# A one-token difference of attention values by way of DRAM, with regrouped stores of a triangular inverse

## The chip, the cores and the metric

The kernel runs on one NeuronCore of one Trainium2 chip. Its engines each work through a queue of their own in order: PE (TensorE, matmul), DVE (VectorE), ACT (ScalarE), POOL (GpSimd) and SP (SyncE). DMAs are issued from the queues of SP, ACT and POOL. The metric is the device time of one launch in microseconds, as the median of several runs. A profile is one execution of its own, taken by the hardware profiler.

## The reference

One layer of a decoder trunk on a sequence of 1024 tokens, width 1024, all in float32. One projection of the normalised input feeds three branches, whose gated sum goes through an output projection and then a feed-forward block with a short causal convolution:

```python
h = rms_norm(x, norm1_g)
p_rwkv, p_sb, q_mem, gate_logits = split(h @ w_in)
y_a = rwkv7_branch(p_rwkv, ...)            # delta-rule recurrence, 8 heads of 64
y_b = stick_breaking_branch(p_sb, ...)     # causal attention, 8 heads of 64
y_m = memory_branch(q_mem, mem, ...)       # attention into 256 memory tokens
x = x + (sum over branches of sigmoid(gate) * (y @ w_branch)) @ w_out
x = x + conv_ffn(x)
```

In the second branch the weight of an earlier token is a product over the tokens between; with `z = q k / 8` the reference computes

```python
attn = where(mask, exp(log_sigmoid(z) + log_between), 0)
out  = attn @ v
```

The weights of one query sum to one less a running product of `sigmoid(-z)`. So the kernel doesn't form the weights but the running product itself, and multiplies it with the differences of neighbouring values, `v[t-1] - v[t]`; the value of the last token of each block of 128 is added at the end as a bias. These differences, and these last values, are what the change is about.

## The kernel before

**Matmul in three products.** Each operand that must be exact is split into a rounded part and a rest (`split_w`, `split_raw`): ACT writes the rounded part (L80), POOL the rest (L81), and PE runs three products (`mm3`, all recorded at L112, the line of the helper `mmul`; transposes are at L105). Weights come in tiles of 128x1024 (`wr`, L76, two buffers, from SP's queue), with two buffers each for the parts `wh` and `wl`.

**The order of the work.** `run` weaves a main stage with a stream of filler items. `items` is a list of generators; `stream` starts each one (its weight load and split) one item ahead and then steps through it. `weave` steps the main stage and draws fillers at a ratio. PE's instructions stay in the order in which they are written (`pinned`); the other engines' orders are set by a scheduler under priorities. The main stages are: `rwkv_prep(p)` for the four head pairs p, `sb_attn`, `mem_attn`, `stage2` (the recurrence), `group_norm`. After them come the output projection, the up phase and the down phase, whose products fill PE.

**Around the values.** While `rwkv_prep(3)` runs, the fillers are the eight items of `sb_v`: for two halves `jg` of the sequence and four weight tiles `kt`, 24 products each. After `kt == 3` ACT writes four blocks of 128 tokens x 512 columns to two tiles `raw` (tag `w4`, three buffers; L655), two token blocks e = 0, 1 to a tile. `differ(i, raw)` then makes the difference tile `v[i]` (tag `A`, four buffers): L622 copies rows 0 to 126 of `raw` to rows 1 to 127 of `v`, from SBUF to SBUF; L623 and L625 copy the single row 127 to row 0 of the next block; L626 stores row 127 to the DRAM tensor `vld`; and on DVE L627 subtracts `raw`. `load_vlast` (L668) brings the last values back as eight DMAs of single numbers, one for each half of the partitions and tile (`jk`), so that ACT can take them as a bias (L868).

In the same stretch `rwkv_prep(3)` needs DVE for its elementwise chains (L384 to L387), for the masked copies of Gram products out of PSUM (`gram`, L401) and for the first steps of the inverse, and PE for the Gram products and for transposes (`turned`, L423). PSUM tiles of tag `g` have four buffers. SP also carries the stores `scr` (L285, L405), `mad` (L409) and `ggd` (L436). POOL brings `mad` back as `inst` (L457).

**The inverse.** `inverse` solves 128 unit triangular systems of 64x64 in place, one to a partition of `X = inst`, in 124 DVE steps (L467, L469) that the fillers draw (`pace`). At the end one DMA from POOL's queue (L472) stores all of `inst` to the DRAM tensor `td`, 16 KB from each partition. The buffer of `inst` is used again for `yhi` (L1091) once that store has read it.

**The recurrence.** `stage2` goes through 16 chunks of 64 tokens, two to a group g. For each group SP loads, for each head pair, a tile of stored operands (`at<-scr`, L490), and for each two pairs a tile `V2` from `vd` (two DMAs, L494) and from `td` (four DMAs, L497, each 64 partitions x 2 x 64 numbers). The fillers there are the gate and branch projections, whose loads (`w<-yd` L1105, `w<-gsd` L1119, `w<-mrd` L1122, `wr`) stand in the same queue of SP.

Of the kernel before, what the change touches and what calls it, by code (L numbers as in the profile page):

```python
# [11 lines left out]
F32 = mybir.dt.float32  # L12
# [3 lines left out]
ALU = mybir.AluOpType  # L16
AX = mybir.AxisListType

T = 1024
# [3 lines left out]
NG = NC // 2  # L23
# [26 lines left out]
class Trunk:  # L50
# [67 lines left out]
    def setup(self):  # L118
        nc, tc = self.nc, self.tc
        E = self.ctx.enter_context  # L120
        self.pool_c = E(tc.tile_pool(name="const", bufs=1))
        self.bufs_p = {"mm": 4, "g": 4}
        self.pool_ps = E(tc.tile_pool(name="psum", bufs=4, space=bass.MemoryType.PSUM))
        self.pool_d = E(tc.tile_pool(name="dram", bufs=1, space=bass.MemoryType.DRAM))
        self.pool_wt = E(tc.tile_pool(name="weights", bufs=2))
        self.pool_s = E(tc.tile_pool(name="small", bufs=2))
        self.kon = self.pool_c.tile([128, NKON], F32, name="kon")
        self.params = self.pool_c.tile([128, NPAR], F32, name="params")
        nc.sync.dma_start(self.params, self.I["params"])

        def kon(n):
            o, w = KON[n]
            return self.kon[:, o : o + w]

        self.ident, self.blk, self.ones = kon("ident"), kon("blk"), kon("ones")
        self.mm_mask, self.ind = kon("mm"), kon("ind")
        self.scr = self.pool_d.tile([4, NG, 128, 1024], F32, name="scr")
        self.mad = self.pool_d.tile([128, 64, 64], F32, name="mad")
        self.vd = self.pool_d.tile([2, 2, NG, 64, 4, 64], F32, name="vd")
        self.td = self.pool_d.tile([128, 64, 64], F32, name="td")  # L140
        self.yd = self.pool_d.tile([3, 4, 128, 1024], F32, name="yd")
        self.mrd = self.pool_d.tile([8, 128, 1024], F32, name="mrd")
        self.gsd = self.pool_d.tile([3, 8, 128, 1024], F32, name="gsd")
        self.x2d = self.pool_d.tile([8, 128, 1024], F32, name="x2d")
        self.vmd = self.pool_d.tile([128, 1024], F32, name="vmd")
        self.vld = self.pool_d.tile([4, 1024], F32, name="vld")
        self.actd = self.pool_d.tile([NF // 2, 7, 128, 512], F32, name="actd")
        self.ggd = self.pool_d.tile([4, 2, 128, 1024], F32, name="ggd")

# [310 lines left out]
    def inverse(self):  # L460
        nc = self.nc
        X = self.inst
        for s in range(1, 63):
            n = 63 - s
            tmp = self.t4("it")
            tv = tmp[:, : s * n].rearrange("p (j t) -> p j t", j=s)
            self.pinned(nc.vector.tensor_tensor(tv, X[:, 0:s, s : s + 1].to_broadcast([128, s, n]), X[:, s : s + 1, s + 1 : 64].to_broadcast([128, s, n]), ALU.mult))  # L467
            yield
            self.pinned(nc.vector.tensor_tensor(X[:, 0:s, s + 1 : 64], X[:, 0:s, s + 1 : 64], tv, ALU.add))  # L469
            yield  # L470
        nc.vector.memset(X.rearrange("p s t -> p (s t)")[:, 0 : 64 * 64 : 65], 1.0)
        nc.gpsimd.dma_start(self.td, X)  # L472

    def stage2(self):
        nc = self.nc
# [5 lines left out]
        hq = [slice(0, 64), slice(64, 128)]  # L481
        heads = [(p, h2) for p in range(4) for h2 in range(2)]
# [4 lines left out]
        def load(g, p, what="LV"):  # L487
            if "L" in what:
                Ls[g, p] = self.t4("at")
                nc.sync.dma_start(Ls[g, p], self.scr[p, g])  # L490
            if "V" in what and p % 2 == 0:
                V2 = self.t4("qk")
                for h2 in range(2):
                    nc.sync.dma_start(V2[hq[h2], h2 * 256 : h2 * 256 + 256], self.vd[p // 2, h2, g].rearrange("s c i -> s (c i)"))  # L494
                td = self.td.rearrange("(p h g c) s i -> p h g s c i", p=4, h=2, g=NG)
                for i, h2 in heads[0:4]:
                    nc.sync.dma_start(V2[hq[h2], 512 + i * 128 : 640 + i * 128].rearrange("s (c i) -> s c i", c=2), td[p + i, h2, g])  # L497
                for i in range(2):
                    VTs[g, p + i] = [V2[:, h2 * 256 + i * 128 : h2 * 256 + i * 128 + 128] for h2 in range(2)], V2[:, 512 + i * 128 : 640 + i * 128]

# [7 lines left out]
        for c in range(NC):  # L508
            g, cc = c // 2, c % 2
# [104 lines left out]
    def sb_v(self):  # L614
        nc = self.nc
        out = {}
        self.v = []
        halves = [slice(0, 512), slice(512, 1024)]

        def differ(i, raw):  # L620
            v = self.v[i]
            nc.sync.dma_start(v[1:128], raw[0:127])  # L622
            nc.sync.dma_start(v[0:1, halves[1]], raw[127:128, halves[0]])  # L623
            if i < 3:
                nc.sync.dma_start(self.v[i + 1][0:1, halves[0]], raw[127:128, halves[1]])  # L625
            nc.sync.dma_start(self.vld[i : i + 1], raw[127:128])  # L626
            nc.vector.tensor_tensor(v, v, raw, ALU.subtract)  # L627

        def item(jg, kt):
            hi, lo = self.split_w(self.I["w_v"][kt])  # L630
            yield
            if kt == 0:
                out[jg] = [self.ps("mm") for _ in range(4)]
            if (jg, kt) == (0, 3):
                self.v += [self.t4("A", n=1024) for _ in range(4)]
                nc.vector.memset(self.v[0][0:1, halves[0]], 0.0)

            def mm(kk, j):
                k = kt * 2 + kk
                w = slice(kk * 512, (kk + 1) * 512)  # L640
                js = slice((jg * 4 + j) * 128, (jg * 4 + j + 1) * 128)
                for pi, (a, b) in enumerate(((self.xhi, hi), (self.xlo, hi), (self.xhi, lo))):
                    self.mmul(out[jg][j], a[k][:, js], b[:, w], start=(k == 0 and pi == 0), stop=(k == 7 and pi == 2))

            for i in range(4):
                for e in range(2):
                    if kt == 3:
                        mm(e, i)
                    else:
                        mm(i // 2, i % 2 * 2 + e)  # L650
                if kt == 3:
                    jj = jg * 4 + i
                    if i % 2 == 0:
                        raw = self.t4()
                    nc.scalar.activation(raw[:, (jj % 2) * 512 : (jj % 2 + 1) * 512], out[jg][i], AF.Copy, scale=self.rsc[:, jj : jj + 1])  # L655
                    if i % 2:
                        differ(jj // 2, raw)
                if i == 1:
                    self.settle()
                yield  # L660

        return [item(jg, kt) for jg in range(2) for kt in range(4)]

    def load_vlast(self):
        self.vlast = self.small("jk", [128, 64], bufs=1)[:, :32].rearrange("c (i u) -> c i u", i=4)
        for i in range(4):
            for e in range(2):
                self.nc.sync.dma_start(  # L668
                    self.vlast[e * 64 : e * 64 + 64, i], self.vld[i, e * 512 : e * 512 + 512].rearrange("(u c) -> c u", c=64))

    def head_norm(self, pst, nh, width, fold, neg=None):
        nc = self.nc
# [133 lines left out]
    def sb_attn(self, qk, need):  # L806
# [40 lines left out]
        def back(u):  # L847
# [13 lines left out]
            if b % 4 == 2:  # L861
                q = slice(h2 * 64, h2 * 64 + 64)
                y = self.t4("ys", n=512)
                for i in range(2):
                    rows = slice(i * 64, i * 64 + 64)
                    for bb in range(2):
                        o = (2 * bb + i) * 128
                        nc.scalar.activation(  # L868
                            y[q, o : o + 128], py[rows, bb * 128 : bb * 128 + 128], AF.Identity,
                            bias=self.vlast[rows, half * 2 + bb, 2 * p + h2 : 2 * p + h2 + 1])  # L870
                nc.scalar.dma_start(self.yd[1, p, q, half * 512 : (half + 1) * 512], y[q])

        for u in range(len(units) + 4):
# [817 lines left out]
    def run(self):  # L1691
# [16 lines left out]
        self.marks = marks  # L1708
        items = [self.shift_item(i + p, krv[p], f"{n}{p}") for p in range(4) for n, i in (("k", 4), ("r", 0), ("v", 8)) if (p, n) != (0, "k")]
        items += self.sb_v()  # L1710
        inv = self.inverse()
        gq = [(b, d) for b in (1, 0) for d in range(8)]
        gq[14:14] = [(2, 0), (2, 1)]
# [2 lines left out]
        mark = lambda name: lambda: marks.add(name)  # L1716
        for p in range(4):
            kp, kss, qp, hooks = self.sb_qk(p, qk[p])
            items += [kp, gate(), kss, qp, gate(hooks), mark(f"sb{p}")]
            if p == 0:  # L1720
                items.append(self.load_vlast)
        prep, mss, mv, mk = self.mem_kv()
        mqi = [None] * 4
        for h in range(4):
# [119 lines left out]
```

## Time and profile before

| | |
|---|---|
| median of 3 runs | 1969.23 us (1967.92 to 1970.93) |
| the profiled execution's own time | 1968.17 us |
| its span in the profile | 1966.4 us |
| mean granted TensorE clock | 0.972 of full speed |
| PE busy | 1836.3 us (93%) |
| PE weight loads busy | 1458.2 us (74%) |
| DVE / ACT / POOL busy | 1167.1 / 886.9 / 775.3 us |
| DMA | 259.19 MB, mean 132 GB/s |

The span is what the profile covers; the time of the execution is 1.77 us longer. PE is busy nearly throughout, so what matters are the stretches where it is not: idle time of an engine that PE doesn't wait for costs nothing. In the rows of a timeline, what stands in square brackets is the idle time of that engine just before the row and what ended it. In the rows of windows each engine has its busy time in the window and the number of its instructions; then come the granted clock, the busy share of the 16 DMA engines and their rate.

### The profile page before, as it was taken

The numbers are of one execution on the slowest core, as the hardware profiler recorded it, in microseconds if no ns is written. First come the engines' busy times: TensorE is split into PE (matmuls) and PEld (weight loads), VectorE is DVE, ScalarE is ACT, GpSimd is POOL, SyncE is SP. The second block draws the span as 40 slices with busy tenths as digits, with TensorE's granted clock in tenths as the row PEclk, the third lists the DMA queues.
The fourth block names the chain that finished last, engine by engine and source line by source line (L and its number), as shares of the span: only waits on it lengthen the run. The fifth ranks groups of instructions, "written<-read, shape, count | busy, mean of one in ns | idle before, by whom it ended". The sixth has DMA issues, their size and how long they took to land. (4 is left out here: it accounts for less than half of the span.)

```text
span 1966.4 us, 27535 instructions
## 1 busy us (share of the span) xinstructions
PE 1836.3 (93%) x10500; PEld 1458.2 (74%) x10500; DVE 1167.1 (59%) x1643; ACT 886.9 (45%) x1665; POOL 775.3 (39%) x432
## 2 busy tenths in 40 slices
PE   8999966499999999999899989989999999999999
PEld 6777755377878788777677768767888888878877
DVE  5756641388888632433423376266767777786496
ACT  5444411246556563553455533454444444445433
POOL 2223321123122233212132353348676767635444
PEclk9999987699999999999899999999999999999999
DMA  4245524211111142166665455322323322377465
GB/s 170 80 146 167 179 93 127 67 46 42 59 38 59 63 159 86 49 219 206 221 218 183 152 182 178 110 96 81 102 85 114 109 95 94 106 272 263 138 223 196
DMA packets 128588, 259.19 MB, mean 132 GB/s; under 512 B 40776, under 2 KB 51272, under 8 KB 128200
## 3 DMA queue, kind: packets, MB, share of 16 engines
q1 hardware_dynamic: 93208, 193.72, 30.2%
q10 hardware_dynamic: 32608, 51.13, 7.4%
q0 software_dynamic: 2640, 12.58, 1.8%
q8 instruction: 82, 1.34, 0.3%
q14 instruction: 50, 0.41, 0.1%
HBM read 176.89 MB, written 78.40 MB: 130 GB/s over the span
## 5 line engine op out<-in xcount | busy, mean ns | idle before, releaser
L81 POOL TENSOR_TENSOR wl<-wr,wh 128x1024 fp32r<-128x1024 f32 x77 | 194.6, 2528 | 616.2 <-ACT wh L80 593.9
L112 PE MATMUL mm<-xhi,wh 128*128 128x512 f32 x784 | 270.2, 425 | 10.0 <-ACT xhi L185 8.3
L112 PE MATMUL mm<-xlo,wh 128*128 128x512 f32 x784 | 250.2, 401 | 0.1
L112 PE MATMUL mm<-xhi,wl 128*128 128x512 f32 x784 | 248.9, 399 | 0.6 <-POOL wl L81 0.6
L112 PEld LDWEIGHTS mm<-xhi,wl 128*128 128x128 f32 x784 | 149.1, 190 | 37.6 <-POOL wl L81 1.3
L112 PEld LDWEIGHTS mm<-xlo,wh 128*128 128x128 f32 x784 | 149.6, 191 | 36.9 <-DVE xlo L186 0.8
L80 ACT ACTIVATE wh<-wr 128x1024 fp32r<-128x1024 f32 x77 | 81.4, 1057 | 197.3 <-PE mm L112 73.1
L112 PEld LDWEIGHTS mm<-xhi,wh 128*128 128x128 f32 x784 | 138.5, 193 | 42.8 <-ACT xhi L185 8.3
L112 PE MATMUL mm<-dw,da 128*128 128x512 f32 x528 | 121.6, 390 | 2.4 <-DVE da L1586 2.2
L112 PE MATMUL mm<-BT,l 128*128 128x512 f32 x504 | 119.9, 393 | 0.0
L112 PE MATMUL mm<-BT,wh 128*128 128x512 f32 x352 | 111.5, 398 | 7.7 <-DVE u L1399 7.7
L833 DVE TENSOR_TENSOR_SCAN at<-at,rbc 128x128 f32<-128x128 f32 (+3 forms) x64 | 91.2, 1426 | 45.2 <-ACT at L827 45.1
L112 PEld LDWEIGHTS mm<-dw,da 128*128 128x128 f32 x528 | 98.8, 188 | 24.5 <-DVE da L1586 3.5
L1587 POOL TENSOR_TENSOR dw<-draw,dw 128x512 fp32r<-128x512 f32 x55 | 80.9, 1479 | 84.5 <-ACT dw L1585 81.6
L112 PE MATMUL mm<-B,wh 128*128 128x512 f32 x352 | 110.4, 395 | 1.6 <-ACT p L1441 1.6
L112 PEld LDWEIGHTS mm<-BT,l 128*128 128x128 f32 x504 | 94.6, 188 | 22.0
L1586 DVE TENSOR_TENSOR da<-draw,da 128x512 fp32r<-128x512 f32 x77 | 65.9, 865 | 59.4 <-ACT da L1584 58.8
L112 PE MATMUL g<-dw,da 128*128 128x512 f32 x396 | 90.8, 390 | 2.3 <-ACT dw L1585 1.2
L1347 POOL TENSOR_TENSOR l<-it,l 128x1024 fp32r<-128x1024 f32 x21 | 50.5, 2407 | 103.3 <-ACT l L1346 103.3
L112 PEld LDWEIGHTS g<-dw,da 128*128 128x128 f32 x396 | 74.2, 188 | 18.4 <-ACT dw L1585 1.6
L1584 ACT ACTIVATE da<-draw 128x512 fp32r<-128x512 f32 x77 | 48.3, 628 | 83.7 <-PE mm L112 39.6
L112 PE MATMUL g<-qk,qk 64*128 64x128 f32 (+2 forms) x448 | 69.6, 329 | 16.6 <-DVE at L401 15.0
(321 smaller groups left out, 4007.1 us busy)
## 6 DMA issues: line engine op xcount, KB each, us to landing
wr<-in_w_in_dram SPq DMA_DIRECT2D x50, 512.0 KB, 3.5
draw<-actd SPq DMA_DIRECT2D x77, 256.0 KB, 3.8
at<-scr SPq DMA_DIRECT2D x32, 512.0 KB, 5.0
draw<-in_w_down_dram SPq DMA_DIRECT2D x55, 256.0 KB, 4.0
wr<-in_w_up_dram SPq DMA_DIRECT2D x22, 512.0 KB, 3.5
actd<-gall ACTq DMA_DIRECT2D x44, 256.0 KB, 2.8
rw<-in_w_up_dram SPq DMA_DIRECT2D x20, 512.0 KB, 3.6
gsd<-w ACTq DMA_DIRECT2D x18, 512.0 KB, 2.7
```

What stands on the lines that cost most here:

```text
L80: self.nc.scalar.activation(hi, raw, AF.Copy)
L81: self.nc.gpsimd.tensor_tensor(lo, raw, hi.bitcast(F32), ALU.subtract)
L112: self.pinned(self.nc.tensor.matmul(*a, **k))
L833: self.pinned(nc.vector.tensor_tensor_scan(sn[:, :W][:, ::-1], sn[:, :W][:, ::-1], self.rbc[:, :W], 1.0, ALU.mult, ALU.bypass))
L1347: nc.gpsimd.tensor_tensor(lo, src, hi.bitcast(F32), ALU.subtract)
L1584: self.pinned(nc.scalar.activation(A[:, 0], a, AF.Copy))
L1586: self.pinned(nc.vector.tensor_tensor(A[:, 1], a, A[:, 0].bitcast(F32), ALU.subtract))
L1587: nc.gpsimd.tensor_tensor(Wt[:, 1], w, Wt[:, 0].bitcast(F32), ALU.subtract)
```

## The change

Three things are changed.

1. `differ` no longer shifts rows within SBUF. Each `raw` tile is stored whole to a DRAM tensor `vsd` of 1025 rows x 512 columns, one row below its place (`vsd[t + 1]`), by one DMA of 128 partitions from ACT's queue. Row 0 is stored as zeros at the start. Later, ahead of the item `kp` of the first head pair, `differ` loads `vsd[t]`, the values one token earlier, by one DMA of 128 partitions for each of the four tiles, and DVE subtracts. The third and fourth `raw` tiles now have the tag `at` (seven buffers); the tiles are held until the subtraction.
2. The last values of the eight blocks are one load of 8 rows of `vsd` (`vl8`), and `spread_last`, behind the gate item that follows `kp`, turns them by 16 small products against the identity and one DVE copy.
3. The inverse's one store becomes 16, of 8 partitions each, into a `td` laid out by group; behind each of them `inverse` yields three times. `stage2` then loads `td` for two head pairs by one DMA of 128 partitions x 256 numbers instead of four.

```diff
-        self.td = self.pool_d.tile([128, 64, 64], F32, name="td")
+        self.td = self.pool_d.tile([2, NG, 2, 64, 2, 128], F32, name="td")
...
-        self.vld = self.pool_d.tile([4, 1024], F32, name="vld")
+        self.vsd = self.pool_d.tile([T + 1, 512], F32, name="vsd")
...
-        nc.gpsimd.dma_start(self.td, X)
+        for p in range(4):
+            for h2 in range(2):
+                for cc in range(2):
+                    i0 = p * 32 + h2 * 16 + cc
+                    nc.gpsimd.dma_start(self.td[p // 2, :, h2, :, p % 2, cc * 64 : cc * 64 + 64], X[i0 : i0 + 15 : 2])
+                    for _ in range(3):
+                        yield
...
-                td = self.td.rearrange("(p h g c) s i -> p h g s c i", p=4, h=2, g=NG)
-                for i, h2 in heads[0:4]:
-                    nc.sync.dma_start(V2[hq[h2], 512 + i * 128 : 640 + i * 128].rearrange("s (c i) -> s c i", c=2), td[p + i, h2, g])
+                nc.sync.dma_start(V2[:, 512:768], self.td[p // 2, g].rearrange("h s p i -> (h s) (p i)"))
...
-        def differ(i, raw):
-            v = self.v[i]
-            nc.sync.dma_start(v[1:128], raw[0:127])
-            nc.sync.dma_start(v[0:1, halves[1]], raw[127:128, halves[0]])
-            if i < 3:
-                nc.sync.dma_start(self.v[i + 1][0:1, halves[0]], raw[127:128, halves[1]])
-            nc.sync.dma_start(self.vld[i : i + 1], raw[127:128])
-            nc.vector.tensor_tensor(v, v, raw, ALU.subtract)
...
-                        raw = self.t4()
+                        raw = self.t4("at" if jg else "w4")
...
-                        differ(jj // 2, raw)
+                        b = jj // 2 * 256 + 1
+                        nc.scalar.dma_start(self.vsd[b : b + 256].rearrange("(e s) c -> s e c", e=2), raw.rearrange("s (e c) -> s e c", e=2))
+                        self.raw.append(raw)
...
-    def load_vlast(self):
-        self.vlast = self.small("jk", [128, 64], bufs=1)[:, :32].rearrange("c (i u) -> c i u", i=4)
-        for i in range(4):
+    def differ(self):
+        nc = self.nc
+        vl8 = self.t4("ys", n=512)
+        for i, raw in enumerate(self.raw):
+            v = self.t4("A")
+            nc.sync.dma_start(v.rearrange("s (e c) -> s e c", e=2), self.vsd[i * 256 : i * 256 + 256].rearrange("(e s) c -> s e c", e=2))
+            nc.vector.tensor_tensor(v, v, raw, ALU.subtract)
+            self.v.append(v)
+        nc.sync.dma_start(vl8[0:8], self.vsd[128 : T + 1 : 128])
+        self.vlast = vl8
+
+    def spread_last(self):
+        nc, vl8 = self.nc, self.vlast
+        self.vlast = self.small("jk", [128, 64], bufs=1)[:, :32]
+        pt = self.ps("g")
+        for u in range(8):
             for e in range(2):
-                self.nc.sync.dma_start(
-                    self.vlast[e * 64 : e * 64 + 64, i], self.vld[i, e * 512 : e * 512 + 512].rearrange("(u c) -> c u", c=64))
+                self.mmul(pt[e * 64 : e * 64 + 64, u * 4 : u * 4 + 4], vl8[0:8, u * 64 : u * 64 + 64], self.ident[0:8, e:8:2], start=True, stop=True)
+        nc.vector.tensor_copy(self.vlast, pt[:, :32])
...
+        zero = self.t4("ys", n=512)
+        nc.vector.memset(zero[0:1], 0.0)
+        nc.sync.dma_start(self.vsd[0:1], zero[0:1])
...
-            items += [kp, gate(), kss, qp, gate(hooks), mark(f"sb{p}")]
-            if p == 0:
-                items.append(self.load_vlast)
+            items += [*([self.differ] if p == 0 else []), kp, gate(), *([self.spread_last] if p == 0 else []), kss, qp, gate(hooks), mark(f"sb{p}")]
```

What the scheduler makes of it is shown at three places, with the rows in the order in which each queue holds them.

SP's queue while `rwkv_prep(3)` runs, before: `w_316` and `w_321` are the first two `raw` tiles, `A_1933` to `A_1935` difference tiles, `qk_1999`, `at_1730` and `at_2078` results of `rwkv_prep`.

```order
L623 DMA A_1933<-w_316_1944 1x16x32
L622 DMA A_1933<-w_316_1944 127x1024
L625 DMA A_1934<-w_316_1944 1x16x32
L626 DMA vld<-w_316_1944 1x1024
L285 DMA scr<-qk_1999 128x4x256
L436 DMA ggd<-at_1730 128x1024
L622 DMA A_1934<-w_321_1983 127x1024
L623 DMA A_1934<-w_321_1983 1x16x32
L625 DMA A_1935<-w_321_1983 1x16x32
L409 DMA mad<-at_2078 64x4x64
```

The same place of SP's queue in the changed kernel; `A_2260` and `A_2263` are the first two difference tiles, `wr_2144` the last weight tile of `sb_v`, `wr_2190` that of `kp`.

```order
L76 DMA wr_2144<-in_w_v_dram 128x1024
L436 DMA ggd<-at_1733 128x1024
L662 DMA A_2260<-vsd 128x2x512
L285 DMA scr<-qk_2107 128x4x256
L405 DMA scr<-at_2068 128x2x512
L409 DMA mad<-at_2068 64x4x64 x2
L405 DMA scr<-at_2090 128x2x512
L409 DMA mad<-at_2090 64x4x64 x2
L76 DMA wr_2190<-in_w_in_dram 128x1024
L662 DMA A_2263<-vsd 128x2x512
```

The shifting copies of 127 rows and of single rows are gone from SP; loads of 128 rows stand in their place, the second of them behind the Gram stores and the weight load of `kp`.

POOL's queue at the end of the inverse, before; `wl` are rests of weights, `rm` a norm factor of the memory branch, `it` the zeroed state of `stage2`.

```order
L81 TENSOR_TENSOR wl_5186<-wr_5183,wh_5185 128x1024
L472 DMA td<-inst 128x4096
L480 MEMSET it_6832 128x512
L81 TENSOR_TENSOR wl_5416<-wr_5413,wh_5415 128x1024
L172 TENSOR_TENSOR rm_5393<-rs_5394,half 128x2
L81 TENSOR_TENSOR wl_5461<-wr_5458,wh_5460 128x1024
L81 TENSOR_TENSOR wl_5502<-wr_5499,wh_5501 128x1024
```

The same place of POOL's queue in the changed kernel.

```order
L81 TENSOR_TENSOR wl_5194<-wr_5191,wh_5193 128x1024
L476 DMA td<-inst 8x64x64 x2
L172 TENSOR_TENSOR rm_5401<-rs_5402,half 128x2
L81 TENSOR_TENSOR wl_5424<-wr_5421,wh_5423 128x1024
L476 DMA td<-inst 8x64x64
L81 TENSOR_TENSOR wl_5470<-wr_5467,wh_5469 128x1024
L81 TENSOR_TENSOR wl_5511<-wr_5508,wh_5510 128x1024
```

One store has become sixteen, of which the first stand here; the others follow among the next thirteen weight rests, and the zeroing of `it` now stands behind the last of them.

SP's queue in `stage2`, at the load of one group, before; `at_7761` and `at_7763` are the operand tiles of the third and fourth head pair, `w_1312` a load for the branch fillers.

```order
L494 DMA qk_7754<-vd 64x256 x2
L497 DMA qk_7754<-td 64x2x64 x4
L1105 DMA w_1312_7657<-yd 128x1024
L490 DMA at_7761<-scr 128x1024
L490 DMA at_7763<-scr 128x1024
L494 DMA qk_7765<-vd 64x256 x2
```

The same place of SP's queue in the changed kernel.

```order
L500 DMA qk_7758<-vd 64x256 x2
L501 DMA qk_7758<-td 128x256
L496 DMA at_7762<-scr 128x1024
L1111 DMA w_1315_7661<-yd 128x1024
L496 DMA at_7764<-scr 128x1024
L500 DMA qk_7766<-vd 64x256 x2
```

Four DMAs of `td` have become one, and one of the two operand loads has moved ahead of the load for the fillers.

More of the change, by code (lines that the diff above doesn't have):

```diff
@@ L616, in sb_v @@
         out = {}
-        self.v = []
-        halves = [slice(0, 512), slice(512, 1024)]
-        def differ(i, raw):
-            v = self.v[i]
-            nc.sync.dma_start(v[1:128], raw[0:127])
-            nc.sync.dma_start(v[0:1, halves[1]], raw[127:128, halves[0]])
-            if i < 3:
-                nc.sync.dma_start(self.v[i + 1][0:1, halves[0]], raw[127:128, halves[1]])
-            nc.sync.dma_start(self.vld[i : i + 1], raw[127:128])
-            nc.vector.tensor_tensor(v, v, raw, ALU.subtract)
+        self.raw = []
         def item(jg, kt):
@@ L633, in item @@
                 out[jg] = [self.ps("mm") for _ in range(4)]
-            if (jg, kt) == (0, 3):
-                self.v += [self.t4("A", n=1024) for _ in range(4)]
-                nc.vector.memset(self.v[0][0:1, halves[0]], 0.0)
             def mm(kk, j):
@@ L866, in back @@
                     for bb in range(2):
-                        o = (2 * bb + i) * 128
+                        o, bi = (2 * bb + i) * 128, (2 * p + h2) * 4 + half * 2 + bb
                         nc.scalar.activation(
                             y[q, o : o + 128], py[rows, bb * 128 : bb * 128 + 128], AF.Identity,
-                            bias=self.vlast[rows, half * 2 + bb, 2 * p + h2 : 2 * p + h2 + 1])
+                            bias=self.vlast[rows, bi : bi + 1])
                 nc.scalar.dma_start(self.yd[1, p, q, half * 512 : (half + 1) * 512], y[q])
@@ L1710, in run @@
         items += self.sb_v()
+        self.v = []
+        zero = self.t4("ys", n=512)
+        nc.vector.memset(zero[0:1], 0.0)
+        nc.sync.dma_start(self.vsd[0:1], zero[0:1])
         inv = self.inverse()
```

## The prediction

> **What bounds the kernel now.** I began with the page: how busy PE is, and where in the 40 slices it isn't.
>
> ```profile
> PE 1836.3 (93%) x10500; PEld 1458.2 (74%) x10500; DVE 1167.1 (59%) x1643; ACT 886.9 (45%) x1665; POOL 775.3 (39%) x432
> ...
> PE   8999966499999999999899989989999999999999
> ...
> PEclk9999987699999999999899999999999999999999
> DMA  4245524211111142166665455322323322377465
> ```
>
> PE is the bound: it idles for only 130 us of the span. Nearly half of that lies in slices 6 to 8, where the granted clock falls too. The view by windows puts it beside the stage ahead of it.
>
> ```profile
> 150.00:200.00 50.00, 48.46 (x290) 37.18 (x289) 33.00 (x44) 21.25 (x26) 15.23 (x7) 1.00 0.58 178
> 200.00:250.00 50.00, 48.05 (x281) 35.95 (x280) 31.06 (x37) 23.07 (x28) 20.27 (x9) 1.00 0.54 170
> 250.00:300.00 50.00, 27.78 (x139) 21.18 (x137) 22.00 (x24) 6.20 (x8) 10.37 (x5) 0.83 0.26 86
> 300.00:350.00 50.00, 36.24 (x160) 28.31 (x160) 5.78 (x8) 7.88 (x11) 7.59 (x4) 0.79 0.41 125
> 350.00:400.00 50.00, 25.89 (x154) 21.02 (x155) 25.10 (x32) 15.89 (x17) 11.43 (x5) 0.69 0.25 72
> ```
>
> From 150 to 250 us (the preparation of the third head pair) PE idles 3.5 us in 100. From 250 to 400 us the same kind of work, for the last pair, leaves every engine idle for long, DVE too. So no engine limits this stretch, something that they all wait for does. PE's timeline names the stops:
>
> ```profile
> 279.96 1.97 PE L105 MATMUL g<-kon,it 128*128 128x128 f32 x8 [10.20 <-DVE at L401]
> 303.02 2.67 PE L112 MATMUL g<-qk,qk 64*128 64x128 f32 x16 [15.05 <-DVE at L401]
> 312.63 0.80 PE L112 MATMUL mm<-wh,xhi 128*128 128x512 f32 x1 [6.94 <-ACT wh L80]
> 315.06 0.79 PE L112 MATMUL mm<-wl,xhi 128*128 128x512 f32 x1 [1.21 <-POOL wl L81]
> 374.11 1.88 PE L112 MATMUL g<-kon,w 128*64 128x2 f32 x32 [26.70 <-ACT w L754]
> ```
>
> Together 60.1 us. DVE's timeline says why L401 came late: it stood behind the subtraction L627.
>
> ```profile
> 301.14 1.23 DVE L627 TENSOR_TENSOR A<-A,w 128x1024 f32<-128x1024 f32 x1 [20.55 <-DMA A<-w]
> ...
> 370.88 1.23 DVE L627 TENSOR_TENSOR A<-A,w 128x1024 f32<-128x1024 f32 x1 [20.43 <-DMA A<-w]
> ```
>
> And SP's own rows, with the DMA view of 245 to 375 us (landing times in the last column, the rate in 40 slices):
>
> ```profile
> 271.10 15.31 SPq L623 DMA_DIRECT2D A<-w  x1
> ...
> 336.77 18.42 SPq L623 DMA_DIRECT2D A<-w  x1
> ```
>
> ```profile
> GB/s 161 9 280 49 25 32 303 142 87 25 25 26 27 45 194 28 26 147 233 311 280 94 6 310 63 216 133 24 27 26 25 25 26 25 122 226 25 26 27 9
> ...
> scr<-at SPq DMA_DIRECT2D x4, 512.0 KB, 3.3
> wr<-in_w_in_dram SPq DMA_DIRECT2D x4, 512.0 KB, 15.7
> ...
> A<-w SPq DMA_DIRECT2D x4, 508.0 KB
> ```
>
> Read together: the shifted copy of 127 rows (508 KB) moves at 25 to 27 GB/s, so in some 20 us, which is what DVE waits; a copy of 128 rows of that size lands in 3.3 us. While it runs, the single-row copy behind it holds SP for 15 to 18 us, and the weight tiles behind that land after 15.7 us. So one slow transfer blocks DVE, SP's queue and, by `wh`, PE.
>
> **The change part by part.** The sum is made on the profiled execution's own 1968.2 us.
>
> *The shifted copies go: -60.1.* With L622, L623, L625, L626 and the 8 loads of `jk` gone, the five stops lose their cause. What is late next is counted below.
>
> *The clock: -8.6.* PE's work right behind a stop ran at a lower granted clock:
>
> ```profile
> 280.00:290.00 10.00, 7.97 (x32) 6.48 (x32) 0.59 (x2) 1.19 (x2) 1.90 (x1) 0.85 0.10 33
> 300.00:310.00 10.00, 2.67 (x16) 2.28 (x16) 3.71 (x5) 0.00 (x0) 0.00 (x0) 0.50 0.72 225
> 310.00:320.00 10.00, 6.16 (x24) 4.28 (x25) 0.83 (x2) 2.80 (x3) 4.67 (x2) 0.50 0.47 127
> 370.00:380.00 10.00, 5.89 (x42) 5.00 (x43) 8.78 (x12) 5.20 (x6) 4.96 (x2) 0.50 0.35 71
> ```
>
> Busy time by what was missing of the clock: 7.97 x 0.15 + (2.67 + 6.16 + 5.89) x 0.5 = 8.6 us. The Trainium skill ("TensorE: Matmul & The Clock Gate", What's actually happening) has the clock at half until some 3.4 us of sustained work have passed; four long stops would then cost 4 x 1.7 = 6.8 us by an estimate from it, and the sum would be 1.8 us higher. The trace speaks for more: the clock stayed at 0.50 through 8.8 us of broken work.
>
> *The new way of the values: +3.5.* Each tile is now stored by ACT and loaded by SP, and DVE's subtraction still stands among the Gram copies. A hand-over's price is bounded by these rows of the page:
>
> ```profile
> at<-scr SPq DMA_DIRECT2D x32, 512.0 KB, 5.0
> ...
> scr<-at ACTq DMA_DIRECT2D x8, 512.0 KB, 6.2
> mrd<-w POOLq DMA_DIRECT2D x16, 512.0 KB, 5.3
> ```
>
> So 6.2 + 5.0 = 11.2 us from store to subtraction. The first two stores follow ACT's rows L655, and their loads stand behind `ggd`, the second also behind the Gram stores and `kp`'s weights:
>
> ```profile
> 252.88 2.02 ACT L655 ACTIVATE w<-mm,rsc 128x512 f32<-128x512 f32 x3 [2.90 <-PE g L105]
> ```
>
> ```profile
> 264.41 5.23 SPq L436 DMA_DIRECT2D ggd<-at  x1
> ```
>
> That is over 10 us from store to load, and only the load is open. I expect DVE to wait for the second some 7 us; behind it stand the last two pairs of Gram copies, and PE needs them only for the transposes, with 24 and then 18 products of `sb_v` ahead of these: at 48.05/281 = 0.17 us each (the window from 200 us) 7 us, so that wait is just covered. The last two loads wait for their stores, and SP holds one weight load behind them; two weight tiles are under way by then, and `kp` and its gate (96 products) cover 16 us. Without that cover DVE's start on the inverse, and PE's first `sb` products behind `spread_last`, would come up to 11 us later. I leave the stretch the 3.5 us per 100 of the stage ahead of it; ends 0 and 44.8 (four hand-overs open), nearer to the first since work is at hand.
>
> *Last values: +0.9.* 16 products by 1.88/32 us each (the row at 374.11 above), with no cover on PE, and a copy of 32 columns on DVE. The store of zeros costs nothing: it lies under the first loads.
>
> *The inverse's stores: +1.* One POOL issue becomes 16, each 512 pieces of 256 bytes. POOL's rows nearest to that, and POOL's load where they go:
>
> ```profile
> L472 POOL DMA_DIRECT2D td<-inst x1: 648/648/648, 695.5 to 695.5; - x1
> ```
>
> ```profile
> L1137 POOL DMA_DIRECT2D mrd<-w x16: 531/571/621, 901.3 to 1157.6; - x16
> ```
>
> ```profile
> 690.00:740.00 50.00, 50.00 (x407) 42.24 (x405) 16.66 (x17) 32.18 (x63) 18.57 (x10) 0.97 0.47 166
> 740.00:790.00 50.00, 50.00 (x322) 41.02 (x321) 15.33 (x29) 18.65 (x37) 17.31 (x10) 1.00 0.22 72
> ```
>
> At 0.65 us a store, 16 take 10.4 us out of the 64.1 us that POOL idles in this 100. PE's cover is that weights are split an item ahead; a norm factor (`rm`, `hf`) that waits behind two or three stores may cost a little, so I take 1 us; the ends are 0 and 8 (four such factors, each 2 us late by three stores). The last store stands, by the order, just ahead of this row of POOL, and the loads of `td` began later:
>
> ```profile
> 803.74 1.64 POOL L172 TENSOR_TENSOR hf<-rs,half 128x8 f32<-128x8 f32 x1 [2.01 <-DVE rs L171]
> ```
>
> ```profile
> L497 SPq DMA_DIRECT2D qk<-td x64: 573/605/1737, 819.9 to 1076.8; - x64
> ```
>
> So they aren't held up, as long as a store lands within 16 us. Moving the zeroing of `it` behind the stores costs nothing, since the recurrence starts after it.
>
> *The recurrence: -5 (+2.2 to -9.5).* SP issues 16 loads of `td` instead of 64. There PE waits for operand tiles that stand behind them:
>
> ```profile
> PE g L112 <- DMA at<-scr: 9.5, 5, 4.6
> ```
>
> ```profile
> 955.88 0.48 PE L112 MATMUL g<-it,at 64*64 64x64 f32 x4 [4.64 <-DMA at<-scr]
> ...
> 988.28 0.33 PE L112 MATMUL g<-it,at 64*64 64x64 f32 x4 [2.19 <-DMA at<-scr]
> ```
>
> Three issues fewer ahead of a tile can cover the wait of 2.19 us; at 955.88 the tile stood behind `w<-yd`, which itself waited for a buffer, and only one of two tiles moves ahead of it. About half of 9.5 is my choice; an order that puts another load late could cost one more wait of 2.2.
>
> Sum: 1968.2 - 60.1 - 8.6 + 3.5 + 0.9 + 1 - 5 = 1899.9. The median of the runs shown is 1.1 above the profiled execution, hence 1901.
>
> **The rivals.**
>
> *The DRAM way stalls as the copies did.* If all four hand-overs lie open on DVE and PE follows, 44.8 us come back in place of 3.5: 1942. For it: DVE works in order and both the second and the last two loads come late on SP. Against it: the stores precede by long, and PE has products at hand. Chance 0.08.
>
> *POOL falls behind (slower than before).* If POOL must work for each store in proportion to its pieces, the 5.3 us to landing of a `mrd` store of 128 rows bounds one of 512 pieces at 4 x 5.3 = 21.2 us; 16 are 339 us, less 64.1 us of POOL's idle time, and PE waits for the weights' rests: 1901 + 275 = 2176. It delays PE from 64.1/16 = 4.0 us a store, and the kernel is slower than before from (64.1 + 68)/16 = 8.3 us. Against it: POOL's issue took 0.65 us for 2048 KB and 0.57 for 512 KB. Chance 0.03. The Trainium skill ("SBUF — State Buffer", A bandwidth-pool intuition that's wrong) speaks against stores from POOL: DVE can lock it out of writing descriptors, about 620 ns then becoming 3100. Its 16 x 3.1 = 49.6 us would still fit POOL's idle time by an estimate; the 16 `mrd` rows, beside a busy DVE, show at most 0.62 us.
>
> *The 127 rows aren't the cause* (any transfer there would be as slow), and nothing is gained: 1969. Against it stand the 3.3 us of `scr<-at` in the same window. Chance 0.02.
>
> **How the numbers follow.** The forecast has 0.87. Its own bounds: the recurrence at its best and no idle time left give 1901 - 4.5 - 3.5, and fewer stops there give back some of the clock that it lacks (the 8 in slice 20 of PEclk: over a tenth of 49 us, say 6): 1887. At the other end, 15 us of idle time left, stores at 8, the recurrence at no gain: 1901 + 11.5 + 7 + 5 = 1924.5. The first rival and the others lie outside, 0.13. Faster by over 0.2% (about 4 us, what a measurement of this kernel can tell from no change): 0.87 + 0.08 = 0.95; the same 0.02; slower 0.03.
>
> **What would show it.** In the new profile: no `A<-w`; `A<-vsd` landing in 4 to 8 us; slices 6 to 8 of PE at 9 with a full clock; PE's stops from 250 to 330 us below 6 us in sum; SP never held for over 10 us by one row there; POOL's `td` rows below 1 us each; PE's waits for `at<-scr` at about half. I am wrong if DVE's subtraction still waits over 10 us with PE idle behind it, if the clock stays low without stops, or if `td` rows on POOL take several us and `wl` starts to hold PE.

## The result, and the profile after

The changed kernel takes 1897.32 us (median of 4 runs, 1895.29 to 1907.12), beside 1968.58 us for the kernel before (4 runs, 1966.14 to 1970.93): a ratio of 0.9648, 95% interval 0.9613 to 0.9683. The forecast was 1901 us, with a range of 1887 to 1924. The profiled execution took 1896.67 us (span 1894.9 us).

Page of the changed kernel:

```profile
PE 1825.7 (96%) x10532; PEld 1451.2 (77%) x10532; DVE 1170.7 (62%) x1644; ACT 886.9 (47%) x1665; POOL 789.3 (42%) x447
...
PE   8999999999999999998999899979999999999998
...
PEclk9999999999999999999999999999999999999999
DMA  4255564211112441566744462322333232386475
```

The hole in slices 6 to 8 is gone, and the clock's dip with it. The windows of the stretch:

```profile
250.00:300.00 50.00, 47.59 (x257) 36.82 (x256) 31.34 (x31) 14.34 (x20) 19.76 (x9) 1.00 0.78 248
300.00:350.00 50.00, 49.02 (x301) 38.91 (x299) 39.29 (x50) 21.66 (x27) 19.44 (x9) 1.00 0.31 95
350.00:400.00 50.00, 49.66 (x333) 39.60 (x332) 43.06 (x38) 31.39 (x57) 11.07 (x5) 1.00 0.13 43
```

How much of the gain lies there? The first attention output (`ys`, the eviction with the last values as bias) marks the end of the stretch in both kernels. From the start of the span to it, before and after:

```profile
0.00:430.10 430.10, 352.15 (x1863) 269.89 (x1863) 232.86 (x279) 156.51 (x194) 115.45 (x54) 0.91 0.39 123
```

```profile
0.00:363.00 363.00, 344.76 (x1901) 264.53 (x1901) 236.53 (x281) 156.69 (x194) 116.77 (x54) 0.99 0.48 151
```

The mark comes 67.1 us earlier. PE's idle time ahead of it falls from 77.95 to 18.24 us, by 59.7; its busy time falls by 7.4, though 38 more instructions stand there. Everything behind the mark gives 4.4 us more (71.5 by the spans).

DVE still waits, now for the loads from DRAM, 24.4 us in four waits. Its timeline shows the two longest (the last column is the idle time before the row):

```profile
284.38 3.22 DVE L663 TENSOR_TENSOR A<-A,w 128x1024 f32<-128x1024 f32 x1 [7.67 <-DMA A<-vsd]
300.52 1.25 DVE L663 TENSOR_TENSOR A<-A,at 128x1024 f32<-128x1024 f32 x1 [10.52 <-DMA A<-vsd]
```

and PE hardly notices; these are its two largest stops between 250 and 330 us:

```profile
272.03 1.26 PE L105 MATMUL g<-kon,it 128*128 128x128 f32 x8 [0.97 <-DVE at L401]
288.35 1.16 PE L105 MATMUL g<-kon,it 128*128 128x128 f32 x8 [1.44 <-DVE at L401]
```

The DMA view of 245 to 375 us shows each half of the hand-over (the store to `vsd`, the load to `A`), and weights that land in 3.7 us where they took 15.7:

```profile
wr<-in_w_in_dram SPq DMA_DIRECT2D x9, 512.0 KB, 3.7
A<-vsd SPq DMA_DIRECT2D x4, 512.0 KB, 5.9
...
vsd<-w ACTq DMA_DIRECT2D x2, 512.0 KB, 3.9
```

### The profile page after: what moved, and what is told of

Read it like the earlier page. It is cut to its first block, busy times and chain, and to the rows that moved or that the text cites. A ratio compares the mean times of both kernels' runs of the same rounds, so it can differ in the third digit from the quotient of the medians.

```text
span 1894.9 us, 27535 instructions
## 1 busy us (share of the span) xinstructions
PE 1825.7 (96%) x10532; PEld 1451.2 (77%) x10532; DVE 1170.7 (62%) x1644; ACT 886.9 (47%) x1665; POOL 789.3 (42%) x447
## 5 line engine op out<-in xcount | busy, mean ns | idle before, releaser
L1592 DVE TENSOR_TENSOR da<-draw,da 128x512 fp32r<-128x512 f32 x77 | 64.8, 851 | 60.7 <-ACT da L1590 60.1
L738 DVE TENSOR_TENSOR w<-w,rbc 128x1024 f32<-128x1024 f32 x24 | 50.6, 2108 | 69.6 <-ACT w L737 62.5
L112 PE MATMUL g<-dw,da 128*128 128x512 f32 x396 | 90.8, 390 | 2.4 <-ACT dw L1591 1.3
```

What stands on the lines that cost most here:

```text
L112: self.pinned(self.nc.tensor.matmul(*a, **k))
L738: nc.vector.tensor_tensor(g, g, self.rbc, ALU.mult)
L1592: self.pinned(nc.vector.tensor_tensor(A[:, 1], a, A[:, 0].bitcast(F32), ALU.subtract))
```

## The experiments

Each time is compared with runs of the kernel before on the same chip. Twelve kernels were run.

**split_copy**: the kernel before, with the same way within SBUF but other row counts.

```diff
-            nc.sync.dma_start(v[1:128], raw[0:127])
+            nc.sync.dma_start(v[1:113], raw[0:112])
+            nc.sync.dma_start(v[113:128], raw[112:127])
```

> The kernel before, with one line changed: the copy of 127 rows from SBUF to SBUF (L622) is issued as two copies, of 112 and of 15 rows. The single-row copies, the store to vld and the eight small loads of the last values stay. Theory: what blocked the stretch from 250 to 400 us is that a copy of 127 rows goes through one DMA engine (25 to 27 GB/s), since 127 rows don't divide among 16. Then both pieces land in some 4 us, DVE's subtractions wait under 8 us instead of 20.5, the single rows behind them no longer hold SP for 15 us, and the time falls by 50 to 68 us, to 1900 to 1918. Rival, the route: any copy within SBUF with its rows shifted, or the single-row copies and the small loads, would block as long; then the time stays above 1955. A middle value (1920 to 1950) would say that the single rows or the small loads carry a part of their own.

1910.74 us, ratio 0.971 (0.9691 to 0.9729): 57 us are gained without DRAM. The pieces in the DMA view:

```profile
A<-w SPq DMA_DIRECT2D x4, 448.0 KB, 4.2
...
A<-w SPq DMA_DIRECT2D x4, 60.0 KB, 4.9
```

PE's timeline from 250 to 400 us has 11.3 us of stops left, 60.1 before. The longest is one late weight:

```profile
285.88 0.79 PE L112 MATMUL mm<-wh,xhi 128*128 128x512 f32 x1 [5.11 <-ACT wh L80]
```

So the row count was the cause of most of it. What is left for the route, the single rows, the eight small loads and the new handling of the inverse together is some 12 us by the ratios (0.971 beside 0.9643 to 0.9648 for the changed kernel).

**load_127**: the reverse, the changed kernel's route with the old row count.

```diff
-            nc.sync.dma_start(v.rearrange("s (e c) -> s e c", e=2), self.vsd[...])
+            nc.sync.dma_start(v3[0:127], d3[0:127])
+            nc.sync.dma_start(v3[127:128], d3[127:128])
```

> The changed kernel, with each load of 128 rows of A from vsd issued as two, of 127 rows and of one. Theory (the number of rows decides, not the route): the load of 127 rows from DRAM runs at 25 to 27 GB/s too, lands after some 20 us, the subtractions wait for about that long, and the last two loads one after the other hold up the weights of the next items; the time rises by 15 to 50 us over the changed kernel, to 1912 to 1947. Rival (the way within SBUF was slow, DRAM is fast for any number of rows): within 3 us of the changed kernel, 1894 to 1900.

1963.95 us, ratio 0.999 (0.9975 to 1.0006). The row count decides, but the price was more than the 15 to 50 us expected: all of the gain is lost. DVE waits 99.6 us in all for the four loads, and behind three of them the issue of the single-row load holds SP for 17 to 21 us. The first of these, and PE's stops, from their timelines:

```profile
294.08 17.06 SPq L664 DMA_DIRECT2D A<-vsd  x1
```

```profile
299.49 1.94 PE L105 MATMUL g<-kon,it 128*128 128x128 f32 x8 [14.15 <-DVE at L401]
325.56 1.22 PE L112 MATMUL mm<-xhi,wh 128*128 128x512 f32 x2 [12.14 <-ACT wh L80]
334.18 1.22 PE L112 MATMUL mm<-xhi,wl 128*128 128x512 f32 x2 [6.54 <-POOL wl L81]
378.08 1.87 PE L112 MATMUL g<-kon,ys 8*64 8x4 f32 x32 [32.00 <-DMA ys<-vsd]
```

The Trainium skill ("DMA: Bandwidth & Descriptors", Why a DMA increments its semaphore by 16 and not by 1) has the rule: a transfer uses the largest number of DMA engines up to 16 that divides the slowest dimension of both its sides, so 127 rows take one. No view here counts the engines, but the times agree: 112 and 15 rows land in 4.2 and 4.9 us, while DVE waits some 20.5 us for a copy of 127 rows (before) and 21.0 to 32.2 us for a load of 127 (load_127).

**late_subtract** and **late_pinned**: by which way did the slow copy reach PE? The copies of the kernel before stay; DVE's subtractions move behind the Gram copies. The edit of late_pinned:

```diff
-            nc.vector.tensor_tensor(v, v, raw, ALU.subtract)
+            self.raw.append(raw)
...
+    def late(self):
+        for v, raw in zip(self.v, self.raw):
+            self.pinned(self.nc.vector.tensor_tensor(v, v, raw, ALU.subtract))
...
-            items += [kp, gate(), kss, qp, gate(hooks), mark(f"sb{p}")]
+            items += [*([self.late] if p == 0 else []), kp, gate(), kss, qp, gate(hooks), mark(f"sb{p}")]
```

(late_pinned pins the Gram copies L401 too; in both runs the third and fourth `raw` tiles have the tag `at`.)

> The kernel before, with its copies of 127 rows within SBUF as they are; only the four subtractions (L627) are moved to the place ahead of the item kp, where the changed kernel has them (the third and fourth raw tile take the tag at, as there). SP's queue is blocked as before, DVE is not held among the Gram copies any more. Theory (two ways from the slow copy to PE, each with a price of its own): the stops behind DVE's Gram copies, 10.20 + 15.05 us, go, the others stay or come later, 1930 to 1950. Rival 1, DVE is the only way that counts: 1900 to 1915. Rival 2, SP's queue alone sets the stretch (weights and single rows behind the copies come as late as before): over 1958.

1971.2 us, ratio 1.0019 (1.0006 to 1.0033). This run had the edit without `pinned`, and the scheduler put the second subtraction back among the Gram copies, where it still waited 20.55 us. So the run says nothing about the question.

> In late_subtract the scheduler had put the subtractions back among the Gram copies, so that it tested nothing. Here they and the Gram copies (L401) are pinned in DVE's queue, and all four subtractions stand behind the last Gram copy; the copies of 127 rows stay on SP as before. Theory (the slow copy reaches PE by two ways, DVE and SP's queue): the stops of 10.20 and 15.05 us behind Gram copies go, the weights still come late, 1930 to 1950. Rival 1, DVE alone: 1900 to 1915. Rival 2, SP's queue alone (Gram's own stores and weights stand behind the copies, so PE is held just as long): over 1958.

1966.3 us, ratio 0.9998 (0.998 to 1.0016). PE's timeline:

```profile
272.36 1.26 PE L105 MATMUL g<-kon,it 128*128 128x128 f32 x8 [0.94 <-DVE at L401]
311.25 0.80 PE L112 MATMUL mm<-wh,xhi 128*128 128x512 f32 x1 [31.03 <-ACT wh L80]
313.68 0.79 PE L112 MATMUL mm<-wl,xhi 128*128 128x512 f32 x1 [1.21 <-POOL wl L81]
372.69 1.88 PE L112 MATMUL g<-kon,w 128*64 128x2 f32 x32 [26.53 <-ACT w L758]
```

The stops behind DVE are gone (0.94 us in place of 10.20 and 15.05), and the stop for the weight grew from 6.94 to 31.03 us. The four rows sum to 59.7 us, beside 60.1 before. SP's queue shows why: the store behind the copy is held, and the weight for 311 us is issued only at 305.61.

```profile
271.37 1.31 SPq L622 DMA_DIRECT2D A<-w  x1
272.77 15.26 SPq L285 DMA_DIRECT2D scr<-qk  x1
...
305.61 0.36 SPq L76 DMA_DIRECT2D wr<-in_w_v_dram  x1
```

In the kernel before that weight was issued at 306.21, nearly the same time, though partly by another way. There SP itself waited for DVE, at a store of Gram copies (SP's waits from 240 to 420 us: total, times, longest):

```profile
SPq L409 <- DVE at L401: 10.7, 1, 10.7
```

So the ways cross: the copy held SP, and DVE, held by the same copy, held SP again. In late_pinned the last Gram copy ahead of the weight ends at 281.54, before SP comes to its stores at 288.13 (some stores stand in another order), and the queue alone makes the weight as late.

**copy_unread**: the opposite, the changed kernel with a slow transfer in SP's queue whose data nobody needs.

```diff
                         self.raw.append(raw)
+                        nc.sync.dma_start(self.vxd[jj // 2, 0:127], raw[0:127])
```

> The changed kernel, and beside its new way of the values a store of rows 0 to 126 of each raw tile to a DRAM tensor that nobody reads, from SP's queue, where the kernel before had its shifted copies. No engine needs its data; only the queue and the DMA engine are taken. If SP's queue is one of the ways by which a copy of 127 rows holds PE (what stands behind it is issued 15 us late, the weights among it): 1915 to 1945. If it held PE only by the data that DVE waited for: within 4 us of the changed kernel.

1960.1 us, ratio 0.9965 (0.9949 to 0.9981): nearly the whole gain is lost, again more than expected. SP is held behind the transfers, and the loads and weights behind them come late. DVE waits 90.8 us in all for the late loads, but PE's two long stops name a weight and the load of the last values, both from SP's queue. SP's timeline, then PE's:

```profile
251.86 12.48 SPq L652 DMA_DIRECT2D vxd<-w  x2
264.44 20.86 SPq L286 DMA_DIRECT2D scr<-qk  x1
```

```profile
303.44 0.80 PE L112 MATMUL mm<-wh,xhi 128*128 128x512 f32 x1 [26.57 <-ACT wh L80]
...
369.18 1.87 PE L112 MATMUL g<-kon,ys 8*64 8x4 f32 x32 [30.53 <-DMA ys<-vsd]
```

What no run separates is the queue and the DMA engines behind it: beside the unread transfers the two `vsd<-w` stores from ACT's queue land late too, in 10.6 us (median), 3.9 in the changed kernel.

**copies_pool**: the kernel before, with its copies issued from another queue.

```diff
-            nc.sync.dma_start(v[1:128], raw[0:127])
+            nc.gpsimd.dma_start(v[1:128], raw[0:127])
```

(and so for the three other transfers of `differ`)

> The kernel before, with the shifting copies, the single rows and the stores to vld (L622 to L626) issued from POOL's queue instead of SP's. Theory A (a copy of 127 rows runs through one DMA engine whichever queue issues it): the copies land after some 20 us as before, DVE's waits stay, only the stops through the weights (6.94 + 1.21 us) and what SP's blocking adds go, 1940 to 1965. Theory B (POOL's queue cuts the copy up in another way): the copies land in under 8 us and 45 to 65 us are gained, 1901 to 1921.

1904.71 us, ratio 0.9683 (0.9662 to 0.9703), as theory B had it. From POOL's queue the same 127 rows land in 6.5 us:

```profile
A<-w POOLq DMA_DIRECT2D x4, 508.0 KB, 6.5
```

The same section of the Trainium skill's page has an exception for some direct copies issued from POOL, which spread 127 rows over all 16 engines. The 6.5 us agree with it.

**load_at_once**: the hand-overs of the values laid open.

```diff
-                        self.raw.append(raw)
+                        v = self.t4("A")
+                        nc.sync.dma_start(v.rearrange("s (e c) -> s e c", e=2), self.vsd[...])
+                        nc.vector.tensor_tensor(v, v, raw, ALU.subtract)
+                        self.v.append(v)
```

(The loop over the tiles in `differ` goes.)

> The changed kernel, with each load of A from vsd and its subtraction placed right behind the store of the same tile, where the kernel before had its copies. So all four hand-overs (store, load, subtraction) lie open on DVE, about 4.4 + 5.9 us each by the landing times of the changed kernel, and SP waits for the store in each. The prediction's first rival, that PE follows DVE there: 44.8 us less the 3.5 of the forecast, 1938 for a changed kernel of 1897. The forecast's mechanism, that PE has products of sb_v and kp at hand: DVE waits 30 to 45 us in all, PE loses 5 to 20 of them, 1902 to 1917.

1894.79 us, ratio 0.9628 (0.9613 to 0.9642). Neither came: DVE waits less than in the changed kernel (24.4 us there), as the view of waits has it (total, times, longest):

```profile
DVE A L652 <- DMA A<-vsd: 17.3, 3, 15.6
```

One wait of 15.56 us lies open before the third subtraction, and PE's stops from 250 to 400 us are 3.7 us in sum, as in the changed kernel. So DVE can stand idle there for 15 us at no price to PE.

**values_only** and **td_only**: the change in two parts, the values (with one store and four loads of `td` as before) and the inverse's stores and loads alone.

> The changed kernel with the old handling of the inverse: one store of td of 128 partitions, four loads of td for two head pairs and group. Theory A (the sixteen spaced stores on POOL cost the memory attention the 6 us that the changed kernel gives back there, and the merged loads win some 3 us in the recurrence): 1894, 2 to 4 us faster than the changed kernel. Theory B (the give-back comes from the shifted start of that stage, not from the stores): the stops at the memory attention stay, the recurrence loses its 3 us, 1900. Either way at least 64 of the 71 us stand without the new handling of the inverse.

> The kernel before with the new handling of the inverse alone (sixteen spaced stores, one load of td for two head pairs and group). Theory A (the stores cost the memory attention 6 us, the loads win 3 us in the recurrence): 1971, 1 to 4 us slower than before. Theory B (the stores cost nothing): 1965, 2 to 5 us faster than before. The prediction's own sum for this part was +1 - 5 = -4 us.

values_only took 1902.44 us, ratio 0.9667 (0.9648 to 0.9686), so 65 us of the gain come with the values; its interval overlaps that of the changed kernel. td_only took 1966.0 us, ratio 0.999 (0.9977 to 1.0003): between 4.5 us faster and 0.6 us slower than before, no effect that can be told. Both times fit theory B better than theory A. But the memory attention (shown with the next run) is 58.5 us in values_only and 64.7 in td_only, so its 6 us come with the new stores and the yields between them.

**stores_together**: the sixteen stores without the yields between them.

```diff
                     nc.gpsimd.dma_start(self.td[...], X[i0 : i0 + 15 : 2])
-                    for _ in range(3):
-                        yield
```

> The changed kernel with the sixteen stores of td issued one behind the other (the three yields behind each are gone, so the inverse has 124 steps to be drawn, as before, instead of 172). Theory A (spacing matters): POOL is held for 16 x 0.81 = 13 us in one piece, the rests of the weights behind it come late, and PE loses 3 to 10 us, 1900 to 1907. Theory B (the spacing buys nothing; its 48 added steps only move filler work from the attention to the memory attention): within 3 us of the changed kernel, with attention and memory attention each as long as before the change.

1895.35 us, ratio 0.9632 (0.9618 to 0.9646), as theory B had it. In the memory attention (first to last `rc`, eight softmax sums) the changed kernel and this one show:

```profile
L1058 DVE RECIPROCAL rc<-sm x8: 169/178/180, 711.5 to 776.3; 128x4 f32<-128x4 f32 x8
```

```profile
L1056 DVE RECIPROCAL rc<-sm x8: 165/178/179, 719.8 to 778.4; 128x4 f32<-128x4 f32 x8
```

That is 64.8 us with the yields and 58.6 without; before the change it was 58.6. The attention ahead of it (first to last `ys`) is the other way round:

```profile
L874 ACT ACTIVATE ys<-mm,jk x64: 348/357/365, 363.0 to 661.7; 64x128 f32<-64x128 f32 x64
```

```profile
L872 ACT ACTIVATE ys<-mm,jk x64: 348/358/365, 361.2 to 668.9; 64x128 f32<-64x128 f32 x64
```

That is 298.7 us with and 307.7 without; before the change it was 307.1. So the 48 added steps change which stage the filler work is drawn in, and no effect on the time is shown.

**both** and **changed_again**: the two edits of load_at_once and stores_together in one kernel, beside the changed kernel itself on the same chip.

> The changed kernel with the loads of A right behind their stores (as load_at_once) and the sixteen stores of td without yields between them (as stores_together). Each alone was 1 to 2 us faster than the changed kernel by the ratios to before (0.9628 and 0.9632 beside 0.9648), within what the measurement can tell. If the two are separate gains: 1892 to 1894; if both were chance: within 2 us of changed_again.

> The changed kernel itself, beside the other three on the same chip, so that differences of a few us can be told: 1895 to 1899.

They took 1895.44 us, ratio 0.963 (0.9604 to 0.9657), and 1897.79 us, ratio 0.9643 (0.9622 to 0.9664). The intervals overlap: no version that beats the changed kernel is shown.

## Why the prediction was right, and where it was not

**The shifted copies (-60.1, with +3.5 idle left over): the size was right.** It made -56.6 us of PE's idle time; -59.7 came. That 127 rows from SP's queue are the cause is shown by split_copy, load_127 and copies_pool together.

**The way to PE was only half of it.** The step that does not hold is "DVE's timeline says why L401 came late: it stood behind the subtraction L627", as the reason for 10.20 + 15.05 us of the five stops. The row is read rightly, but these 25 us don't hang on it alone: late_pinned takes the subtractions out of the way and gains nothing, and copy_unread, where no subtraction needs the slow transfer, loses nearly everything. The slow transfer held SP's queue, which makes the weights as late by itself; DVE's wait ran beside that, held SP once more, and ended at about the same time. The sum came out since the change took away both waits at once. By the prediction's reading a change that freed DVE alone would gain those 25 us; late_pinned, which does that, shows no gain (ratio 0.9998). The reverse, SP's queue freed with DVE still waiting some 20 us, was not run.

**The clock (-8.6) and the 16 products (+0.9): right.** The two make -7.7 us of PE's busy time, and -7.4 came ahead of the first `ys`, with the granted clock at 1.00 in all three windows.

**The hand-over: right.** DVE waits 7.67 us for the second load (7 were expected), and PE's products cover it. The first rival (1942 us) needs PE to follow DVE; neither here nor with the open 15.56 us of load_at_once does it. Behind a longer wait it does: in load_127 DVE waits 25.33 us for the first load, and PE stops for 14.15.

**The inverse's stores (+1) and the recurrence (-5): not shown by the times.** The two make -4 us; behind the first `ys` 4.4 us were gained in this pair of profiles, and td_only's interval holds both that and nothing, so the agreement may be luck. The sixteen stores cost POOL more than the 16 x 0.65 us of the sum (busy time and mean ns, from the groups by line), with no price that stores_together shows:

```profile
L476 POOL DMA_DIRECT2D td<-inst x16 | 13.7, 855 | 2.2 <-DVE inst L469 2.2
```

The -5 was half of what PE waits for `at<-scr`. That wait, in two profiles of the same changed kernel (the second is changed_again):

```profile
PE g L112 <- DMA at<-scr: 8.3, 3, 4.7
```

```profile
PE g L112 <- DMA at<-scr: 2.1, 2, 1.4
```

A term that differs by 6 us between two executions of one program can't be read from one of them. The profiles of all the runs together say more: in the six kernels with four loads of `td` this wait is 8.1 to 10.0 us and the recurrence (first to last `ys<-g`) 206.5 to 211.6 us; in the eight with one load they are 2.1 to 8.3 and 203.1 to 208.1. So the stage gains 3 us in the mean, of the sign forecast and somewhat less than 5; the ranges overlap, and no run's time shows it.

**The signs that were named.** `A<-vsd` lands in 5.9 us (4 to 8 said), PE's slices are at 9, and its stops from 250 to 330 us are 2.6 us in sum (below 6 said). Three did not come as put. The longest row of `td` on POOL took 1.30 us, over the 1 us said. "SP never held for over 10 us by one row" fails on a row that harms nobody, three weight loads that wait for free buffers:

```profile
300.71 14.68 SPq L76 DMA_DIRECT2D wr<-in_w_in_dram  x3
```

And PE's waits for `at<-scr`, 8.3 us in this profile, are not at half of 9.5.

## What to carry to other kernels

When an engine waits for a slow transfer and the queue that issued it is held as well, take each wait away by itself before giving it a price: the wait that the trace names may only run beside another that is as long. Give a large transfer on SP's queue a row count that was fast here (112 + 15 rows, or 128 by another way), or issue it from POOL's queue, since one transfer of 127 rows on SP's queue held what stood behind it for 9 to 21 us. A gain of a few us that is read from stages or waits of a single profile needs a second profile of the same kernel first.

## What was not expected of the hardware

- The same copy of 127 rows takes some 20 us from SP's queue (the wait of DVE) and lands in 6.5 us from POOL's.
- Behind a 127-row transfer SP's queue held the next issue for 9 to 21 us, whatever it was: a single row (15.31 us before), a store of 128 rows (15.26 us in late_pinned), a load of 128 rows (19.63 us in copy_unread). A transfer whose data no engine needs costs nearly as much as one that DVE waits for (1960.1 and 1963.95 us).
- An issue of 512 pieces of 256 bytes on POOL took 0.86 us on average, beside 0.65 us for the one of 128 pieces of 16 KB.
